# Mixer of a decoder layer: zero products in the first loads, powers of C ahead in the list, and the value projection on split operands in pieces between the scores

## The chip, the cores and the metric

The kernel runs on one core of a Trainium2 chip. The metric is the device time of one execution in microseconds (us). The kernel before takes 971.11 us as the median of three runs (968.80 to 971.95).

Engines are named as in the profile: PE is TensorE, with PEld for its weight loads, DVE is VectorE, ACT is ScalarE, POOL is GpSimd, and SP issues the loads (SPq is its queue).

## The reference

One decoder layer on 256 tokens of 1024 channels, all in float32. Cut to what matters here:

```python
z = x @ w_in                      # 1024 -> [u 512 | q 512 | k 512 | v 512]
# head group A: diagonal complex state space model, 32 groups x 16 channels, 64 states each
lam_bar = exp(lam * dt);  b_bar = ((lam_bar - 1) / lam) * b
states  = scan(a = lam_bar, b = b_bar . u)            # over the 256 tokens
y       = Re(c . states) + d * u
y       = gelu(y);  y = y * sigmoid(y @ w_glu)        # w_glu 512 x 512
# head group B: causal attention, 8 heads x 64
p       = softmax(mask(q k^T / 8))
att     = p @ v
# both groups through one output projection, then residual + layer norm
h       = layernorm(alpha * x + concat(y, att) @ w_out)
# second sublayer (PEER: product-key choice among 128 x 128 one-neuron experts, then their
# values) and a second layernorm: not touched by the change
```

## The kernel before

The work is one stream of instructions per engine. The source writes the mixer (the first 150 us) as short routines, and the list `CFG["order"]` (L46) says in which order they are called: `u`, `q`, `k`, `va`, `vb` are the four projections of x, `par`, `b`, `c0`, `c`, `rt`, `rot` prepare the state space model on DVE, `min` transposes a prepared matrix on PE, `e0`, `e1` are the products that feed the scan, `s0`, `s1` the scan itself, `a0` and `a1` one step each of the attention for the first and the second 128 tokens, `kin`, `o0`, `o1` the products behind the scan, `p0`, `p1` the attention's values, `glu` the gate. A scheduler then places the instructions on each engine, by the order in which they were written and by when it reckons each to be ready, so that routines mix on an engine.

**Products.** A float32 product on PE is two passes, which the trace shows as two records. For the large products the kernel splits an operand into a rounded part `hi` and the rest `lo` (`split`, L67 to L73: a cast on ACT, L71, and a subtraction on DVE, L72) and adds three products of the split parts, one record each. The four projections of x (`tokproj` L158, its products L164; `chproj` L167, its products L175) use plain float32 products; `w_glu` and `w_out` are split.

**Buffers.** Loads of 512 KB go through rings: `raw` (4 buffers), `hi` (3) and `lo` (3), tags that the projections' weight tiles `w` take in turn (L143 to L151). The PSUM banks are in three rings: `pbank`, `sbank` (two banks; names psb) and `abank` (pa).

**The start.** SP issues the small parameters, two of eight channel tiles of x, the first weights and so on (L130 to L139). DVE clears a large matrix `Bbd` (L564) and computes a long chain of small instructions on 128x16 elements. PE begins with `u`.

**Around the scores.** `e0` writes two sbank banks and `e1` two abank banks (L413). DVE ends the ladder of rotations `rot` (L371 to L376), reads the banks (L421 to L426) and scans (L429). PE goes from `e1` to the first half of the value projection (`va`: 8 products of 128x512), then the scores: per head a score (L520) and a mask (L524), a maximum on DVE (L526), an exponential on ACT (L529), a transpose on PE (L534) and a copy on ACT (L536). The second half of the value projection (`vb`) stands among the transposes of the second 128 tokens. Its two sums are copied to `vn` (L587), and `kin` follows (L395).

**The gate.** `glu` multiplies by split `w_glu` (L475 to L477) with the split input `yh` (ACT, L467) and `yl` (DVE, L468), half by half; the output projection (L654) begins with the attention's channels k = 4 to 7 and fills gaps. `w_out` tile 5 is read through the ring like 4 and 6; tiles 0 and 1 take the places `Kin` and `qk` when these are free (L668).

Of the kernel before, what the change touches and what calls it, by code (L numbers as in the profile page):

```python
# [8 lines left out]
F32 = mybir.dt.float32  # L9
F32R = mybir.dt.float32r  # L10
# [31 lines left out]
def f32(ap):  # L42
    return ap.bitcast(F32)


CFG = dict(order='mask zero u par b q min rt rot k e0 e1 s0 va a0 a0 a0 a0 s1 a1 a1 a1 a1 vb c0 c kin p0 o0 p1 o1 glu',  # L46
           glu='VV',
           post='VV',
           yt='AAAAVVVVVVVPVVVV',
# [4 lines left out]
def layer(ctx, tc, I, out, tap=None, upto=None):  # L54
    nc = tc.nc
    V, S, P, PE = nc.vector, nc.scalar, nc.gpsimd, nc.tensor

    const = ctx.enter_context(tc.tile_pool(name="const", bufs=1))
    stream = ctx.enter_context(tc.tile_pool(name="stream", bufs=1))
    RAWB, HIB, LOB = 4, 3, 3  # L60

    def load(src):
        raw = stream.tile([128, 1024], F32, tag="raw", bufs=RAWB, name="raw")
        nc.sync.dma_start(raw, src.rearrange("p a b -> p (a b)") if len(src.shape) == 3 else src)
        return raw

    def split(raw, eng=V, hi=None, lo=None):  # L67
        if hi is None:
            hi = stream.tile([128, 1024], F32R, tag="hi", bufs=HIB, name="hi")
            lo = stream.tile([128, 1024], F32R, tag="lo", bufs=LOB, name="lo")  # L70
        S.copy(hi, raw)  # L71
        eng.tensor_tensor(lo, raw, f32(hi), op=OP.subtract)  # L72
        return hi, lo  # L73
# [26 lines left out]
    def pbank(shape):  # L100
        return ps.tile(shape, F32, tag="w", bufs=4, name="pw")

    def sbank(shape):
        return ps.tile(shape, F32, tag="s", bufs=2, name="psb")
# [6 lines left out]
    with ExitStack() as px:  # L111
# [6 lines left out]
        with ExitStack() as mx:  # L118
# [8 lines left out]
            prm = se.tile([128, 1088], F32, name="prm")  # L127
            x0 = const.tile([128, 2, ND * T], F32, tag="x2", name="x0")
            xT = x0[:, 0].rearrange("p (d t) -> p d t", t=T)
            nc.sync.dma_start(prm[:, 0:48], I["prm"][:, 0:48])  # L130


            for q in range(4):
                nc.sync.dma_start(xT[:, 2 * q:2 * q + 2], I["xT"][:, 2 * q:2 * q + 2, :])
                if q == 0:
                    w0 = stream.tile([128, 1024], F32, tag="raw", bufs=RAWB, name="raw")
                    for k in range(2):
                        nc.sync.dma_start(w0[:, 512 * k:512 * k + 512], I["w_in"][0, :, k, :])
            nc.sync.dma_start(prm[:, 48:], I["prm"][:, 48:])  # L139
            ahead = {(0, 0): w0}  # L140
            spot = [0]

# [1 line left out]
            def w_in(blk, q):  # L144
                if (blk, q) in ahead:
                    return ahead[blk, q]
                t, n = (("raw", RAWB), ("hi", HIB), ("lo", LOB))[spot[0] % 3]
                spot[0] += 1
                w = stream.tile([128, 1024], F32, tag=t, bufs=n, name="w")
                nc.sync.dma_start(w, I["w_in"][blk, :, 2 * q:2 * q + 2, :].rearrange("p a b -> p (a b)"))  # L150
                return w  # L151


            U = se.tile([128, NPAIR, 2, 32], F32, name="U")
            Uv = U.rearrange("p a b c -> p a (b c)")
            qk = sb.tile([128, 2, 4, T], F32, name="qk")

            def tokproj(blk, pt, qs=range(4)):  # L158
                for q in qs:
                    w = w_in(blk, q)  # L160
                    for k in range(2):
                        d = 2 * q + k
                        for b in range(2):
                            PE.matmul(pt[b], xT[:, d, 128 * b:128 * b + 128],  # L164
                                      w[:, 512 * k:512 * k + 512], start=d == 0, stop=d == 7)

            def chproj(blk, scale):  # L167
                pt = [pbank([128, 2, T])[:, 0] for _ in range(4)]
                for q in range(4):
                    w = w_in(blk, q)  # L170
                    for k in range(2):
                        d = 2 * q + k
                        for m in range(4):
                            c = slice(512 * k + 128 * m, 512 * k + 128 * m + 128)
                            mm = PE.matmul(pt[m], w[:, c], xT[:, d], start=d == 0, stop=d == 7)  # L175
                for m in range(4):
                    S.activation(qk[:, blk - 1, m], pt[m], AF.Copy, scale=scale)
                return mm


            pw = sb.tile([128, 40, NPAIR], F32, name="pw")
# [162 lines left out]
            def s5_min():  # L344
                for ri in range(2):
                    for a in range(4):
                        pt = sbank([128, 4, 128])
                        for i in range(4):
                            PE.transpose(pt[:, i], Bbd[:, ri, 4 * a + i].rearrange("p j g -> p (j g)"),
                                         ident)  # L350
                        S.copy(MinT[:, ri, 4 * a:4 * a + 4], pt)

            def s5_c0():
                for i in range(2):
# [204 lines left out]
            M = {}  # L559
            zx = sb.tile([128, 2, NPAIR, NCH], F32, tag="zx", name="zx") if "P" in CFG["post"] else None  # L560

            def do(w):
                if w == "zero":
                    V.memset(Bbd, 0.0)  # L564
                    P.memset(Cbd, 0.0)
                    P.memset(Rt[:, :, 0:1], 0.0)
                    S.activation(Kin, ident[:, None, :].to_broadcast([128, NPAIR, 128]), AF.Copy,
                                 scale=0.0)
                elif w == "u":
                    pu = [abank([128, 512]) for _ in range(2)]  # L570
                    tokproj(0, pu)
                    for b in range(2):
                        V.transpose(U[:, :, b, :], pu[b].rearrange("p (a g) -> p a g", g=32))
                elif w == "q":
                    M["q"] = chproj(1, 0.125)
                elif w == "k":
                    chproj(2, 1.0)
                elif w == "va":

                    pv = M["pv"] = [sbank([128, 512]) for _ in range(2)]  # L580
                    tokproj(3, pv, range(2))
                elif w == "vb":
                    pv = M["pv"]
                    tokproj(3, pv, range(2, 4))
                    M["v"] = vn = sb.tile([128, 2, 512], F32, tag="vn", name="vn")
                    for b in range(2):
                        S.copy(vn[:, b], pv[b])  # L587
                elif w == "par":
                    M["p"] = s5_params()
                elif w == "b":  # L590
                    s5_b(M["p"][0])
                elif w == "c0":
                    s5_c0()
                elif w == "c":
                    s5_c()
                elif w == "rt":
                    s5_rt(M["p"][1])
                elif w == "rot":
                    s5_rot()
                elif w == "min":  # L600
                    with tc.issue_after(M["q"].ins):
                        s5_min()
                elif w == "kin":
                    s5_kin()
                elif w in ("e0", "e1"):
                    M[w] = s5_e(int(w[1]))
                elif w in ("s0", "s1"):
                    if "S" not in M:
                        M["S"] = sb.tile([128, 2, NPAIR, NCH + 1], F32, tag="MinT", name="Sst")
                        P.memset(M["S"][:, :, :, 0:1], 0.0)  # L610
                    s5_scan(int(w[1]), M["e" + w[1]], M["S"])
                elif w in ("o0", "o1"):
                    if "y" not in M:
                        M["y"] = se.tile([128, 4, 2, 4, 32], F32, tag="yT", name="yT")
                    s5_out(int(w[1]), M["S"], M["y"])
                elif w == "mask":
                    masks()
                elif w in ("a0", "a1"):
                    if w not in M:
                        M[w] = attend(int(w[1]))  # L620
                    next(M[w])
                elif w in ("p0", "p1"):
                    values(int(w[1]), M["v"])
                elif w == "glu":
                    glu(M["y"])
                else:
                    raise ValueError(w)
# [28 lines left out]

            W = {}
            for k in (4, 5, 6, 7):
                if k in LATE:
                    r = W3[:, 2 * (k - 6):2 * (k - 6) + 2]  # L660
                    W[k] = split(load(I["w_out"][:, k, :]), V, r[:, 0], r[:, 1])
                else:
                    W[k] = wload(I["w_out"][:, k, :])
                for b in range(1 if k in LATE else 2):
                    out_mm(b, k, W[k])


            for k, t in enumerate(("Kin", "qk")):  # L668
                r = sb.tile([128, 2, 1024], F32R, tag=t, name="W0")
                W[k] = split(load(I["w_out"][:, k, :]), V, r[:, 0], r[:, 1])  # L670
            W2 = sb.tile([128, 4, 1024], F32R, tag="Bbd", name="W2")
            for k in range(2):
# [548 lines left out]
```

## Time and profile before

| | us |
|---|---|
| median of three runs | 971.11 (968.80 to 971.95) |
| profiled execution | 973.51 |
| its span | 971.7 |
| PE busy in the span | 949.5 (98%), mean granted clock 0.984 |
| DVE busy | 705.2 (73%) |
| ACT busy | 546.6 (56%) |
| scores and value projection, from the end of `e1` to the start of `kin` | 60.03 to 97.35 |
| `kin` | 97.35 to 104.46 |

The times of rows are from one profiled execution of 973.51 us, 2.4 above the median. The start of a row is counted from the span's start. A clock of 1.00 is the higher of PE's two levels, 2.4 GHz, and 0.50 the lower, 1.2 GHz. Idle time in square brackets is what an engine waited before the row, and on what. PE is busy or nearly so in almost every slice of the page, so its own work, its clock and its few waits make the time.

### The profile page before, as it was taken

What the parts mean: (1) busy time and instruction counts of PE and PEld (TensorE: products, weight loads), DVE (VectorE), ACT (ScalarE), POOL (GpSimd) and SP (SyncE); (2) the same over time, 40 slices, a digit from 0 to 9 for tenths busy, and PEclk for the clock granted to TensorE, in tenths of its full rate; (3) what the DMA queues carried; (4) which work ended last, traced back from release to release, by engine and by line L of the source; (5) the groups of instructions that cost most, each with busy time, mean ns of one, the idle gap of its engine ahead of it and who ended that gap; (6) DMA issues with size and microseconds to landing.
All of it is one profiled execution on the core that took longest, in us unless ns stands there. A gap on an engine that the chain in (4) does not pass through costs nothing.

```text
span 971.7 us, 15703 instructions
## 1 busy us (share of the span) xinstructions
PE 949.5 (98%) x5774; PEld 825.5 (85%) x5774; DVE 705.2 (73%) x1495; ACT 546.6 (56%) x1059; POOL 21.4 (2%) x25
## 2 busy tenths in 40 slices
PE   7999999999999999999999999999999999999995
PEld 3876977998888888999999999788888878888884
DVE  8974467999888876987889886555555555555556
ACT  3214353557557557987878775455555565555552
POOL 3000003000000000000000000000000000000002
PEclk9996999999999999999999999999999999999998
DMA  8320283356565565444545444566656575656651
GB/s 336 120 66 16 72 264 125 110 182 192 190 192 188 187 193 187 159 158 152 163 141 166 159 154 155 171 197 193 193 194 195 195 264 193 194 194 195 196 195 43
DMA packets 49788, 166.20 MB, mean 171 GB/s; under 512 B 5296, under 2 KB 9392, under 8 KB 49584
## 3 DMA queue, kind: packets, MB, share of 16 engines
q1 hardware_dynamic: 49712, 165.20, 52.6%
q8 instruction: 45, 0.74, 0.3%
q14 instruction: 31, 0.25, 0.1%
HBM read 163.09 MB, written 2.10 MB: 170 GB/s over the span
## 4 chain that ended last, share of the span: by engine, by line
PE 93%; DVE 4%; DMA 1%; issue 1%; ACT 0%; SPq 0%; DVEq 0%; ACTq 0%
PE pw L1068 35%; PE psb L1141 19%; PE pw L864 11%; PE pw L866 6%; PE pw L1016 3%; PE pw L175 3%; PE pa L1141 2%; PE pw L654 2%; PE psb L164 2%; PE pw L867 2%; PE pw L520 1%; PE pa L164 1%; PE pw L395 1%; DMA w<-in_w_in 1%; PE psb L449 1%; DMA tail<-in_ln_g 1%
## 5 line engine op out<-in xcount | busy, mean ns | idle before, releaser
L72 DVE TENSOR_TENSOR lo<-raw,hi 128x1024 fp32r<-128x1024 f32 x195 | 238.4, 1223 | 155.7 <-ACT hi L71 151.4
L71 ACT CAST hi<-raw 128x1024 fp32r<-128x1024 f32 x195 | 205.0, 1052 | 210.9 <-PE pw L1068 162.3
L1068 PE MATMUL pw<-hi,wh 128*128 128x512 f32 x492 | 151.7, 389 | 1.4 <-ACT wh L985 1.4
L1068 PE MATMUL pw<-hi,wl 128*128 128x512 f32 x492 | 152.1, 389 | 0.6 <-DVE wl L986 0.5
L1068 PE MATMUL pw<-lo,wh 128*128 128x512 f32 x492 | 151.9, 389 | 0.0
L1141 PE MATMUL psb<-x,hi 128*128 128x256 f32 x1024 | 133.3, 283 | 0.0
L1141 PEld LDWEIGHTS psb<-x,hi 128*128 128x128 f32 x1024 | 127.4, 192 | 0.0
L864 PE MATMUL pw<-x,hi 128*128 128x512 f32 x448 | 113.5, 392 | 0.0
L1068 PEld LDWEIGHTS pw<-hi,wh 128*128 128x128 f32 x492 | 92.2, 188 | 21.2 <-ACT wh L985 2.3
L1068 PEld LDWEIGHTS pw<-hi,wl 128*128 128x128 f32 x492 | 92.2, 188 | 20.5 <-DVE wl L986 1.5
L1068 PEld LDWEIGHTS pw<-lo,wh 128*128 128x128 f32 x492 | 92.4, 188 | 19.3
L864 PEld LDWEIGHTS pw<-x,hi 128*128 128x128 f32 x448 | 84.2, 188 | 16.4
L79 DVE TENSOR_TENSOR lo<-raw,hi 128x1024 fp32r<-128x1024 f32 x64 | 78.0, 1219 | 15.2 <-ACT hi L78 14.5
L1010 ACT ACTIVATE o<-eq,gL 128x128 f16<-128x128 f16 x256 | 85.4, 438 | 1.0 <-DVE eq L1006 0.9
L1141 PE MATMUL psb<-x,lo 128*128 128x256 f32 x512 | 76.5, 292 | 0.0
L866 PEld LDWEIGHTS pw<-x,lo 128*128 128x128 f32 x512 | 69.8, 190 | 5.0
L866 PE MATMUL pw<-x,lo 128*128 128x256 f32 x512 | 71.4, 282 | 0.0
L78 ACT CAST hi<-raw 128x1024 fp32r<-128x1024 f32 x64 | 67.4, 1054 | 3.7 <-PE pa L1141 2.3
L1141 PEld LDWEIGHTS psb<-x,lo 128*128 128x128 f32 x512 | 65.1, 191 | 0.0
L869 ACT COPY ul<-pw 128x256 f32<-128x256 f32 x64 | 23.8, 371 | 64.4 <-PE pw L867 64.4
L1023 DVE TENSOR_TENSOR act<-pw,act 128x256 f32<-128x256 f32 x124 | 38.3, 350 | 25.6 <-PE pw L1016 25.5
L985 ACT CAST wh<-act 128x256 fp32r<-128x256 f32 x123 | 51.5, 419 | 0.8 <-PE pw L1068 0.8
(310 smaller groups left out, 1166.7 us busy)
## 6 DMA issues: line engine op xcount, KB each, us to landing
raw<-in_u SPq DMA_DIRECT2D x128, 512.0 KB, 3.5
raw<-in_v SPq DMA_DIRECT2D x128, 512.0 KB, 3.5
w<-in_w_in SPq DMA_DIRECT2D x15, 512.0 KB, 8.2
raw<-in_w_q SPq DMA_DIRECT2D x12, 512.0 KB, 3.7
raw<-in_w_out SPq DMA_DIRECT2D x8, 512.0 KB, 4.1
raw<-in_w_q SPq DMA_DIRECT2D x8, 256.0 KB, 3.8
x<-in_xT SPq DMA_DIRECT2D x4, 256.0 KB, 4.8
raw<-in_w_glu SPq DMA_DIRECT2D x2, 512.0 KB, 3.7
```

The costliest lines, as they stand in the source:

```text
L71: S.copy(hi, raw)
L72: eng.tensor_tensor(lo, raw, f32(hi), op=OP.subtract)
L78: S.copy(hi, raw)
L79: return hi, lo, V.tensor_tensor(lo, raw, f32(hi), op=OP.subtract)
L164: PE.matmul(pt[b], xT[:, d, 128 * b:128 * b + 128], w[:, 512 * k:512 * k + 512], start=d == 0, stop=d == 7)
L864: PE.matmul(pt, hi[:, 128 * d:128 * d + 128], x2[:, d], start=d == 0, stop=False)
L866: PE.matmul(pt[:, 0], lo[:, 128 * d:128 * d + 128], xh[:, d], start=False, stop=False)
L985: S.copy(wh, of_tile(half, i))
L1010: S.activation(o2[:, 1, i // 2, :, i % 2], eq[:, i // 2, :, i % 2], AF.Copy, scale=gL[:, t0 + i:t0 + i + 1])
L1023: V.tensor_tensor(a, gp[:, :, HALF // 2 * h:HALF // 2 * h + n], a, op=OP.mult)
L1068: PE.matmul(acc[b][c], x[:, tk], w[:, 512 * c:512 * c + 512], start=first and j == 0, stop=last and j == 2)
L1141: PE.matmul(pt, w[:, 128 * d:128 * d + 128], x[:, d], start=n == 0 and d == 0, stop=n == 2 and d == ND - 1)
```

## The change

Six edits, all in the mixer. From the first expert product on, PE's order is the same but for names.

- **Zero products.** DVE clears a 128x512 tile `warm` ahead of everything, and PE multiplies it twice into a bank that nothing reads, ahead of `u`. The loads are put in another order: one tile of x, half of the first weights, the parameters, the next tile, the other half, then x and the weights in turn; the larger part of the parameters comes after them.
- **`c0 c` (powers of C)** stand ahead of `e0` in the list rather than behind `vb`.
- **`xs`** splits x (four casts on ACT, four subtractions on DVE) and the weights of the value projection (four casts, four subtractions L72).
- **`v`** is called eight times, between the steps of the attention, and each call adds six products of split operands (L212), for two sums of 128x512. The 16 plain products go.
- **`w_out` tile 5** gets the buffer of `qk`, and tiles 0 and 1 other places.
- The splits of `w_glu`, which stood among the projections, come later on DVE.

```diff
-CFG = dict(order='mask zero u par b q min rt rot k e0 e1 s0 va a0 a0 a0 a0 s1 a1 a1 a1 a1 vb c0 c kin p0 o0 p1 o1 glu',
+CFG = dict(order='mask zero u par b q min rt rot k c0 c xs e0 e1 s0 v v a0 v a0 v a0 a0 v s1 a1 v a1 v a1 a1 v kin p0 o0 p1 o1 glu',
...
-            nc.sync.dma_start(prm[:, 0:48], I["prm"][:, 0:48])
-            for q in range(4):
-                nc.sync.dma_start(xT[:, 2 * q:2 * q + 2], I["xT"][:, 2 * q:2 * q + 2, :])
-                if q == 0:
-                    w0 = stream.tile([128, 1024], F32, tag="raw", bufs=RAWB, name="raw")
-                    for k in range(2):
-                        nc.sync.dma_start(w0[:, 512 * k:512 * k + 512], I["w_in"][0, :, k, :])
-            nc.sync.dma_start(prm[:, 48:], I["prm"][:, 48:])
+            w0 = stream.tile([128, 1024], F32, tag="raw", bufs=RAWB, name="raw")
+            warm = se.tile([128, 512], F32, tag="yT", name="warm")
+            V.memset(warm, 0.0)
+            pt = pbank([128, 512])
+            for _ in range(2):
+                PE.matmul(pt, warm[:, 0:128], warm, start=True, stop=True)
+            for k in range(2):
+                nc.sync.dma_start(xT[:, k], I["xT"][:, k, :])
+                nc.sync.dma_start(w0[:, 512 * k:512 * k + 512], I["w_in"][0, :, k, :])
+                if k == 0:
+                    nc.sync.dma_start(prm[:, 0:48], I["prm"][:, 0:48])
...
+            for q in range(1, 4):
+                nc.sync.dma_start(xT[:, 2 * q:2 * q + 2], I["xT"][:, 2 * q:2 * q + 2, :])
+                ahead[0, q] = w_in(0, q)
+            nc.sync.dma_start(prm[:, 48:], I["prm"][:, 48:])
...
+            def xsplit():
+                for q in range(4):
+                    d = slice(2 * q, 2 * q + 2)
+                    S.copy(mixh[:, d], xT[:, d])
+                    V.tensor_sub(mixl[:, d], xT[:, d], f32(mixh[:, d]))
+                for q in range(4):
+                    own = [se.tile([128, 1024], F32R, tag=t, name="wv") for t in ("yT", "dU")] if q == 2 else ()
+                    with tc.issue_after(M["min"].ins):
+                        M["wv", q] = split(load(I["w_in"][3, :, 2 * q:2 * q + 2, :]), V, *own)
+            def vproj(pt):
+                for q in range(4):
+                    hi, lo = M["wv", q]
+                    for k in range(2):
+                        d, c = 2 * q + k, slice(512 * k, 512 * k + 512)
+                        for b in range(2):
+                            tk = slice(128 * b, 128 * b + 128)
+                            for j, (x, w) in enumerate(((mixh, hi), (mixl, hi), (mixh, lo))):
+                                PE.matmul(pt[b], x[:, d, tk], w[:, c], start=d == 0 and j == 0,
+                                          stop=d == 7 and j == 2)
+                        yield
...
-                elif w == "va":
-                    pv = M["pv"] = [sbank([128, 512]) for _ in range(2)]
-                    tokproj(3, pv, range(2))
-                elif w == "vb":
-                    pv = M["pv"]
-                    tokproj(3, pv, range(2, 4))
-                    M["v"] = vn = sb.tile([128, 2, 512], F32, tag="vn", name="vn")
-                    for b in range(2):
-                        S.copy(vn[:, b], pv[b])
+                elif w == "v":
+                    if "pv" not in M:
+                        M["pv"] = [sbank([128, 512]) for _ in range(2)]
+                        M["vproj"], M["left"] = vproj(M["pv"]), 8
+                    next(M["vproj"])
...
-                if k in LATE:
+                if k == 5:
+                    r = sb.tile([128, 2, 1024], F32R, tag="qk", name="W5")
+                    W[k] = split(load(I["w_out"][:, k, :]), V, r[:, 0], r[:, 1])
+                elif k in LATE:
...
-            for k, t in enumerate(("Kin", "qk")):
-                r = sb.tile([128, 2, 1024], F32R, tag=t, name="W0")
+            for k in range(2):
+                r = sb.tile([128, 2, 1024], F32R, tag="Kin", name="W1") if k else W3[:, 0:2]
```

PE in the kernel before, at the end of `e1` (L413): the plain products of the value projection (L164), then score, mask and score by turns.

```order
L413 MATMUL pa<-U,MinT 128x64 x16
L164 MATMUL psb<-w,x_93 128x512 [waits DMAHW3_49,DVE_49,PE_49]
L164 MATMUL psb<-w,x_93 128x512 [waits DVE_49,PE_49]
L164 MATMUL psb<-w,x_93 128x512 x2
L164 MATMUL psb<-w,x_93 128x512 [waits DMAHW4_49]
L164 MATMUL psb<-w,x_93 128x512 x3
L520 MATMUL pw<-qk 128x128 [waits Activation_49]
L524 LDWEIGHTS identb
L524 MATMUL pw<-mb,identb 128x128
L520 MATMUL pw<-qk 128x128 [waits Activation_49]
```

PE in the changed kernel, at the same place (`e1` is L449, scores L556, masks L560, the value projection L212):

```order
L449 MATMUL pa<-U,MinT 128x64 x16
L556 MATMUL pw<-qk 128x128 [waits Activation_49]
L560 LDWEIGHTS identb
L560 MATMUL pw<-mb,identb 128x128
L556 MATMUL pw<-qk 128x128 [waits Activation_49]
L212 MATMUL psb<-hi,mixh 128x512 [waits DVE_49,PE_49,Pool_49]
L212 MATMUL psb<-hi,mixl 128x512
L212 MATMUL psb<-lo,mixh 128x512
L212 MATMUL psb<-hi,mixh 128x512
L212 MATMUL psb<-hi,mixl 128x512
L212 MATMUL psb<-lo,mixh 128x512
L212 MATMUL psb<-hi,mixh 128x512 [waits DVE_49]
```

The eight plain products are gone from here; the first of the new ones stands two scores behind `e1`, and it waits for DVE, which has to have read the two banks of `e0` (psb) first.

DVE in the kernel before, at the end of the rotations (L375, L376) and at the readings of the banks (L421 to L424):

```order
L375 TENSOR_TENSOR big_116<-rot 128x512
L376 TENSOR_TENSOR rot<-big_115,big_116 128x16x32 [waits DVE_49]
L72 TENSOR_TENSOR lo<-raw,hi 128x1024 [waits DMAHW0_49,DMAHW5_49,PE_49,Activation_49]
L421 TENSOR_TENSOR big_113<-psb,rot 128x512 [waits PE_49]
L425 TENSOR_TENSOR big_116<-psb,rot 128x512 [waits DVE_49]
L422 TENSOR_TENSOR big_114<-psb,rot 128x512 [waits PE_49]
L424 TENSOR_TENSOR big_115<-psb,rot 128x512
```

DVE in the changed kernel, at the same place (rotations L411, L412, readings L457, L458, L460, L461):

```order
L411 TENSOR_TENSOR big_128<-rot 128x512
L72 TENSOR_TENSOR lo<-raw,hi 128x1024 [waits DMAHW4_49,DMAHW2_49,Activation_49]
L412 TENSOR_TENSOR rot<-big_127,big_128 128x16x32 [waits DVE_49]
L72 TENSOR_TENSOR lo<-raw,hi 128x1024 [waits DMAHW6_49,DMAHW5_49,Activation_49]
L72 TENSOR_TENSOR wv<-raw,wv 128x1024 [waits DMAHW6_49,Activation_49]
L457 TENSOR_TENSOR big_125<-psb,rot 128x512 [waits PE_49]
L72 TENSOR_TENSOR lo<-raw,hi 128x1024 [waits DMAHW7_49,DMAHW1_49,Activation_49]
L458 TENSOR_TENSOR big_126<-psb,rot 128x512 [waits DVE_49,PE_49]
L460 TENSOR_TENSOR big_127<-psb,rot 128x512
L459 TENSOR_TENSOR big_125<-big_125,big_126 128x512 [waits DVE_49]
L461 TENSOR_TENSOR big_128<-psb,rot 128x512
```

Four subtractions L72, the splits of the value projection's weights, stand about the end of the rotations and between the readings, where one stood before. Further ahead on DVE, the four subtractions of x stand in the chain of small instructions, ahead of the rotations.

PE in the kernel before, at the second half of the gate (L475 to L477), ahead of it the last products of the output projection (L654) that are ready:

```order
L654 MATMUL pw<-hi,mixh 128x512 x2
L654 MATMUL pw<-hi,mixl 128x512 x2
L654 MATMUL pw<-lo,mixh 128x512 x2
L475 MATMUL psb<-yh,hi 128x256 [waits Activation_49]
L475 MATMUL psb<-yh,hi 128x256
L476 MATMUL psb<-yl,hi 128x256 [waits DVE_49]
L477 MATMUL psb<-yh,lo 128x256
```

PE in the changed kernel, at the same place (gate L511 to L513, output projection L693; W_1078 is the split tile 5):

```order
L693 MATMUL pw<-hi,mixh 128x512 x2
L693 MATMUL pw<-hi,mixl 128x512 x2
L693 MATMUL pw<-lo,mixh 128x512 x2
L693 MATMUL pw<-W_1078,mixh 128x512 x2
L693 MATMUL pw<-W_1078,mixl 128x512
L511 MATMUL psb<-yh,hi 128x256 [waits Activation_49]
L511 MATMUL psb<-yh,hi 128x256
L693 MATMUL pw<-W_1078,mixl 128x512
L693 MATMUL pw<-W_1078,mixh 128x512 x4
L693 MATMUL pw<-W_1078,mixl 128x512
L512 MATMUL psb<-yl,hi 128x256 [waits DVE_49]
L513 MATMUL psb<-yh,lo 128x256
```

Nine products of tile 5 have come to stand about the two waits of the gate's second half, three ahead of the first and six ahead of the second.

## Rows read from the trace of the kernel before

**Rows 1.** The page, the chain that ended last, by engine.

```profile
PE 93%; DVE 4%; DMA 1%; issue 1%; ACT 0%; SPq 0%; DVEq 0%; ACTq 0%
```

**Rows 2.** Windows, the mixer: length, PE, PEld, DVE, ACT, POOL, clock, DMA share, GB/s.

```profile
35.47:40.42 4.95, 4.95 (x39) 4.22 (x38) 4.88 (x14) 4.05 (x9) 0.00 (x0) 1.00 0.34 107
52.94:60.03 7.09, 7.09 (x65) 7.09 (x64) 4.72 (x8) 1.47 (x3) 0.00 (x0) 1.00 0.45 150
60.03:67.05 7.02, 7.02 (x19) 2.91 (x18) 6.76 (x11) 0.00 (x0) 0.15 (x1) 1.00 0.01 1
67.05:70.45 3.40, 3.40 (x19) 2.34 (x18) 1.45 (x3) 1.26 (x6) 0.00 (x0) 1.00 0.52 154
70.45:90.90 20.45, 20.45 (x65) 13.11 (x65) 10.67 (x16) 6.60 (x27) 0.00 (x0) 0.50 0.01 1
97.35:104.46 7.11, 7.11 (x66) 6.91 (x65) 4.30 (x9) 3.23 (x7) 0.00 (x0) 1.00 0.29 84
121.05:128.45 7.40, 5.78 (x35) 4.67 (x35) 6.12 (x15) 6.14 (x10) 0.86 (x1) 1.00 0.77 216
128.45:131.90 3.45, 3.45 (x19) 3.45 (x18) 2.65 (x5) 2.54 (x5) 0.00 (x0) 0.51 0.81 260
```

**Rows 3.** Chain of waits in order of time: start, us, work.

```profile
60.20 6.92 PE psb L164 x16
67.12 0.41 PE pw L520 x2
67.53 0.16 PE pw L524
72.97 1.15 PE pw L520 x4
...
74.13 0.22 PE pw L524
92.40 0.22 PE pa L534 x2
133.67 6.41 PE pw L654 x28
```

**Rows 4.** Timeline of DVE from 28 to 60 us: start, us, instruction, idle before it.

```profile
28.39 0.96 DVE L323 TENSOR_TENSOR Bbd<-big,big 64x768 f32<-64x768 f32 x1
51.17 0.69 DVE L376 TENSOR_TENSOR rot<-big,big 128x512 f32<-128x512 f32 x1
51.78 1.22 DVE L72 TENSOR_TENSOR lo<-raw,hi 128x1024 fp32r<-128x1024 f32 x1
54.87 0.69 DVE L421 TENSOR_TENSOR big<-psb,rot 128x512 f32<-128x512 f32 x1 [1.87 <-PE psb L413]
```

**Rows 5.** Timeline of DVE, PE and its weight loads, the start.

```profile
1.66 3.47 DVE L564 MEMSET Bbd<- 128x4096 f32 x1 [1.66 <-PEq L1210]
5.71 5.32 PE L164 MATMUL pa<-raw,x 128*128 128x512 f32 x8 [5.71 <-DMA raw<-in_w_in]
7.55 0.34 PEld L164 LDWEIGHTS pa<-raw,x 128*128 128x128 f32 x1 [0.52 <-issue]
8.40 0.34 PEld L164 LDWEIGHTS pa<-raw,x 128*128 128x128 f32 x1 [0.52 <-issue]
9.58 0.19 PEld L164 LDWEIGHTS pa<-raw,x 128*128 128x128 f32 x1 [0.24 <-issue]
10.01 0.19 PEld L164 LDWEIGHTS pa<-raw,x 128*128 128x128 f32 x1 [0.24 <-issue]
11.26 10.57 PE L164 MATMUL pa<-w,x 128*128 128x512 f32 x24 [0.23 <-DMA w<-in_w_in]
```

**Rows 6.** Timeline of PE and DVE at the gate's second half.

```profile
125.95 1.23 DVE L72 TENSOR_TENSOR W<-raw,W 128x1024 fp32r<-128x1024 f32 x1
126.70 0.50 PE L475 MATMUL psb<-yh,hi 128*128 128x256 f32 x2 [0.99 <-ACT yh L467]
127.84 0.39 PE L476 MATMUL psb<-yl,hi 128*128 128x256 f32 x1 [0.63 <-DVE yl L468]
```

More of the change, by code (lines that the diff above doesn't have):

```diff
@@ L156, in layer, with tokproj @@
             qk = sb.tile([128, 2, 4, T], F32, name="qk")
-            def tokproj(blk, pt, qs=range(4)):
-                for q in qs:
+            def tokproj(blk, pt):
+                for q in range(4):
                     w = w_in(blk, q)
@@ L178, in chproj @@
                 return mm
+            def xsplit():
[8 more added lines that the diff above has]
+            def vproj(pt):
+                for q in range(4):
+                    hi, lo = M["wv", q]
[7 more added lines that the diff above has]
+                        yield
             pw = sb.tile([128, 40, NPAIR], F32, name="pw")
@@ L350, in s5_min @@
                                          ident)
-                        S.copy(MinT[:, ri, 4 * a:4 * a + 4], pt)
+                        M["min"] = S.copy(MinT[:, ri, 4 * a:4 * a + 4], pt)
             def s5_c0():
@@ L577, in do @@
                     chproj(2, 1.0)
-                elif w == "va":
-                    pv = M["pv"] = [sbank([128, 512]) for _ in range(2)]
-                    tokproj(3, pv, range(2))
-                elif w == "vb":
-                    pv = M["pv"]
-                    tokproj(3, pv, range(2, 4))
-                    M["v"] = vn = sb.tile([128, 2, 512], F32, tag="vn", name="vn")
-                    for b in range(2):
-                        S.copy(vn[:, b], pv[b])
+                elif w == "xs":
+                    xsplit()
+                elif w == "v":
[3 more added lines that the diff above has]
+                    next(M["vproj"])
+                    M["left"] -= 1
+                    if not M["left"]:
+                        M["v"] = vn = sb.tile([128, 2, 512], F32, tag="vn", name="vn")
+                        for b in range(2):
+                            S.copy(vn[:, b], M["pv"][b])
                 elif w == "par":
```

## The prediction

> **What bounds the kernel now.** I read the page first: the chain that ended last is PE for 93% [rows 1], so time can come only out of PE's work, its clock or its waits. I then cut the mixer into windows, since one average hides the stages. Six stretches of those shown run at the higher level; two do not. From 70.45 to 90.90, the scores and transposes, PE is busy all 20.45 us but the clock is 0.50, and 128.45 to 131.90 has 0.51 [rows 2]. The stretch ahead of the first holds scores and masks alone; ahead of the second PE is idle for 1.62 of 7.40 us [rows 2], 0.99 and 0.63 of it in the two waits of the gate [rows 6]. The chain of waits gives prices at both levels: a score of two passes and its mask take 0.41 and 0.16 us at the higher one, two scores and their mask 1.15 and 0.22 at the lower [rows 3].
>
> **The start.** The first product of `u` waits for the loads until 5.71 us, and is first at the lower level: weight loads of 0.34 us follow each other by 0.85 us, later ones of 0.19 by 0.43 [rows 5]. A 128x512 clear of `warm` takes an estimated 0.43 (3.47 for eight times the elements [rows 5]), so the zero products can start at about 2.1 us and are four records of 0.85, to 5.5. If the clock is then up, `u`'s 32 records take 32 x 0.43, some 14 us, and `u` ends at 19.8 where it ended at 21.82 (11.26 and 10.57 [rows 5]). I take 2.0 us earlier; bounds 0 to 2.4. But it does not reach the end, for the reason below.
>
> **DVE ahead of the scores.** The powers of C move in the list, but on DVE they already stood among the rotations; they cost nothing. What comes in is four subtractions of x, 128x512, at 0.60 apart (a row's 0.69 overlaps the next: 51.17 to 51.78 [rows 4]), 2.4 us, and four splits at 1.22 [rows 4], where one was. The clear's 0.43 I put at nothing; at most 0.4. DVE's chain there ran to 53.0 and then waited 1.87 us for `e0` [rows 4]. Now the last rotation, whose end was 51.78, ends 2.4 + 1.2 later, at 55.4; two more splits bring the first reading of a bank to 57.8, where it was 54.87. Behind it come 0.6 for the reading, 1.2 for the fourth split, 0.6 and 0.7 for two more readings: 60.9. Only then is the first bank free for the value projection. PE, 2.0 earlier, ends `e1` at 58.0 (60.03 in the row's edge [rows 2]), does two scores and a mask (1.0) and stands from 59.0. It waits 1.9 us. So the start's gain is spent here, and whether the zeros raise the clock hardly matters. Bounds of the wait: 0, if DVE swallows the subtractions in gaps, to 5, if it has everything, or a load is late. The matrix that PE transposes first was written by 29.35 (28.39 and 0.96 [rows 4]); plus 2.4, that is still ahead of 33.5, when `q` now ends, since PE takes the transposes at 35.47 [rows 2].
>
> **From 60.9 to the end of `kin`.** At the higher level:
> - the value projection, 48 products of one record at 6.41/28 = 0.229 [rows 3]: 11.0. Before, 16 products of two records cost 2 x 6.92 = 13.8 [rows 3];
> - the scores of the first 128 tokens that are left, six at 0.41 + 0.16 and a mask: 3.65;
> - eight heads of the second 128 tokens. No row shows one at the higher level: half of 1.15 + 0.22 is 0.69, two scores of 0.41 and a mask 0.99 [rows 3]; I take 0.80: 6.4;
> - 24 transposes, 0.11 each [rows 3], and up to the 0.20 of an exposed weight load [rows 5]; I take 0.14: 3.4;
> - `kin`, 7.1 [rows 2].
>
> The sum is 31.55, so `kin` would end at 92.45. To this comes the clock. The wait of 1.9 us is longer than the idle time that preceded the fall at 128.45, and that fall lasted 3.45 us [rows 2], half of which is lost: 1.7. In the second 128 tokens, scores and transposes follow each other with one piece of V only; there I count half of another such fall, 0.85. `kin` ends at 95.0 where it ended at 104.46: 9.4 gained.
>
> Is PE still the bound there? DVE's work from 52.94 to 90.90 was 4.72 + 6.76 + 1.45 + 10.67 = 23.6 [rows 2]; from 57.8, with the fourth split, it ends at 82.6, some 2 to 3 us ahead of `kin` on PE. The two splits of `w_glu` and two of `w_out` then fall behind it, 4.9 us beside `kin`'s 7.1, in which DVE had 4.30 busy [rows 2]: about full, but the products behind `kin` need the last of its results only at its end. I charge nothing; up to 1 us if not hidden.
>
> On those transposes a page speaks against me. In rows, 32 of the 39 records from 35.47 to 40.42 are transposes of this kind, and the clock stayed at 1.00 in them and in the next stretch shown [rows 2]. The Trainium skill, "TensorE: Matmul & The Clock Gate", Part 4: PE-mode transpose, says that a transpose does not count as PE work for the clock, so that full speed does not engage. By this rule the clock would not hold among transposes and scores, which is the first rival below; this trace does not agree with it. Also, "Perfetto Trace Analysis" of the Trainium skill, Engine Utilization, halves the output rate for float32 passes; by that a plain 128x512 product would cost 0.46 and the split would lose 3.7 us. The trace has two records of 0.43 for one [rows 3], so it saves 2.8.
>
> **The gate.** PE's first wait in the second half was 0.99 [rows 6]; three products of tile 5 (0.69) now stand ahead of it, which leaves 0.3. The second was 0.63 [rows 6]; `yl` comes 1.2 later, since one more split stands ahead of it on DVE, and six products (1.37) are ahead of it on PE: 0.46. That is 0.86 less idle time, and the products are only brought forward. With half the idle time the fall behind it, 1.7, may go; I count three quarters, 1.3. Together 2.2; bounds 0 (the splits late) to 2.6.
>
> **The sum.** 9.4 + 2.2 = 11.6 us of the profiled execution's 973.5, so 961.9; the median lies 2.4 below that execution, so 959.5. Its own range: 956 (one fall less, the wait half) to 963.5 (a fall more, the gate 1 us).
>
> **The rivals.**
> - *The clock does not hold.* The pieces of V do not keep it up, or a transpose does not count: as much time at the lower level as before, 20.45. For it: before, scores alone let it fall [rows 2]. Against it: V is 11 of 24 us of the stage, spread out, and large products ran at 1.00 wherever PE did not wait. From 92.45, 10.2 are lost: 12.0 - 10.2 + 2.2 = 4.0 gained, 967.1. Chance 13%.
> - *Never a fall.* For it: before `u`'s second weights PE waited too, and went on at 0.43 per record [rows 5]. 12.0 + 2.2 gives 956.9; without the wait 955. 17%.
> - *DVE decides the stage.* It has no gaps for the subtractions, or the weights' splits wait for a load; PE stands 5 us at its first piece, 3.1 more, and a little more of the lower clock: 963. 12%.
> - *Slower: V's products run at the lower level with the rest.* The wait of 1.9 us lets the clock fall, and the mixture does not raise it until `kin`: 24.45 us at the higher level become 48.9, `kin` ends at 116.9, 12.4 late; with 2.2 back at the gate that is 10.2 slower, 981. It decides once more than 14.2 of the 24.45 us (28.4 us in the trace) are at the lower level. Against it: the three stretches of large products at 1.00 [rows 2]. 4%.
> - *No change.* The scores' chain of maximum, exponential and transpose sets the stage, and PE's saved time turns into waits. Against it: PE had no idle time at all in 70.45 to 90.90 [rows 2], and the chain's engines were busy for half of it. 4%.
>
> **How the numbers follow.** The forecast has 50%. A difference under 0.3%, 2.9 us, cannot be told from none here: faster is below 968.2. Faster takes the forecast, 17%, 12% and most of the first rival: 0.89. Within 0.3%: no change and the rest of the first: 0.07. Slower: 0.04. The range for 8 in 10 leaves out the slow case, no change and half of the first rival, and goes down past the case without a fall or a wait: 953.5 to 967.5.
>
> **What would show it.** In the changed kernel's windows, the clock from the first piece of V to `kin`: near 1.00 with one or two falls of some 3 us, or 0.50 for most of it. On PE's timeline, the idle time ahead of the first L212, released by DVE: 1 to 3 us. On DVE's, the first reading (L457) near 57.8. `kin` (L431) ending near 95. At the gate, waits of 0.3 and 0.5 us and no stretch at half clock behind them. At the start, weight loads of 0.19 from the first real product on, and `u` ending near 19.8. I am wrong if `kin` ends after 100, or if the time of the stages behind 155 us differs.

## The result, and the profile after

The changed kernel takes 959.32 us as the median of five runs (958.93 to 960.77), the kernel before 971.01 (968.80 to 971.95). The ratio is 0.9881, with a 95% interval of 0.9869 to 0.9893. The profiled execution took 960.77 us, with a span of 959.0 and a mean clock of 0.996, where before had 0.984.

The windows of the changed kernel, from `e1` to the end of the gate; columns as in [rows 2]:

```profile
51.10:58.31 7.21, 7.21 (x66) 7.12 (x64) 7.21 (x9) 2.34 (x6) 0.00 (x0) 1.00 0.38 106
58.31:59.94 1.63, 1.06 (x6) 0.71 (x6) 1.63 (x4) 0.00 (x0) 0.15 (x1) 0.97 0.92 256
59.94:63.10 3.16, 3.16 (x8) 2.51 (x9) 3.16 (x5) 0.00 (x0) 0.00 (x0) 0.50 0.79 294
63.10:72.28 9.18, 9.18 (x43) 6.17 (x41) 7.50 (x14) 3.51 (x10) 0.00 (x0) 0.99 0.01 2
72.28:80.09 7.81, 7.81 (x42) 5.44 (x41) 7.46 (x11) 3.50 (x15) 0.00 (x0) 1.00 0.01 2
80.09:86.48 6.39, 6.39 (x40) 4.62 (x39) 3.79 (x7) 4.04 (x14) 0.00 (x0) 1.00 0.00 0
86.48:94.62 8.14, 8.14 (x70) 7.21 (x69) 7.14 (x13) 6.08 (x14) 0.00 (x0) 1.00 0.63 192
111.20:120.45 9.25, 8.59 (x50) 6.93 (x49) 7.73 (x16) 7.98 (x12) 0.85 (x1) 1.00 0.80 219
120.45:124.14 3.69, 3.69 (x29) 3.33 (x28) 2.45 (x4) 2.40 (x7) 0.00 (x0) 1.00 0.91 271
```

The 20.45 us at 0.50 of [rows 2] are gone; one stretch of 3.16 us at 0.50 is left, at the first products of V, the value projection. `kin` ends at 94.62 where it ended at 104.46: 9.84 us. In the gate PE is idle for 0.66 us, where it was 1.62 of 7.40 [rows 2], and no stretch at 0.51 follows.

The timeline of PE: the start, the first product of V, and the two waits of the gate.

```profile
1.45 3.78 PE L137 MATMUL pw<-warm 128*128 128x512 f32 x4 [1.45 <-DVE warm L134]
5.03 1.98 PE L174 MATMUL pa<-raw,x 128*128 128x512 f32 x4
7.57 1.95 PE L174 MATMUL pa<-raw,x 128*128 128x512 f32 x4 [0.56 <-DMA raw<-in_w_in]
9.46 10.54 PE L174 MATMUL pa<-w,x 128*128 128x512 f32 x24
...
59.94 0.77 PE L212 MATMUL psb<-hi,mixh 128*128 128x512 f32 x1 [0.57 <-DVE big L460]
60.50 0.63 PE L212 MATMUL psb<-hi,mixl 128*128 128x512 f32 x1
...
116.88 0.50 PE L511 MATMUL psb<-yh,hi 128*128 128x256 f32 x2 [0.28 <-ACT yh L503]
...
119.15 0.39 PE L512 MATMUL psb<-yl,hi 128*128 128x256 f32 x1 [0.38 <-DVE yl L504]
```

The zeros do what they are for: the first real products follow each other by some 0.43 from 5.03 on, where they began at 0.85 [rows 5]. The level is read from this rate alone, since the clock column of the windows has 1.00 at the start of both kernels. But PE then waits for the loads at 7.57, and `u` ends near 19.9 (21.82 before). The first product of V waits 0.57 for DVE. The gate's waits are 0.28 and 0.38 where they were 0.99 and 0.63 [rows 6].

DVE at the readings of the banks:

```profile
53.90 0.69 DVE L412 TENSOR_TENSOR rot<-big,big 128x512 f32<-128x512 f32 x1
54.51 1.22 DVE L72 TENSOR_TENSOR lo<-raw,hi 128x1024 fp32r<-128x1024 f32 x1
55.64 1.22 DVE L72 TENSOR_TENSOR wv<-raw,wv 128x1024 fp32r<-128x1024 f32 x1
56.78 0.69 DVE L457 TENSOR_TENSOR big<-psb,rot 128x512 f32<-128x512 f32 x1
57.38 1.22 DVE L72 TENSOR_TENSOR lo<-raw,hi 128x1024 fp32r<-128x1024 f32 x1
...
59.11 0.68 DVE L460 TENSOR_TENSOR big<-psb,rot 128x512 f32<-128x512 f32 x1
```

The first reading is at 56.78 (54.87 before [rows 4]), and the first bank is free when L460 ends, at 59.8.

### The profile page after: what moved, and what is told of

Same layout as the page of the kernel before. It is cut to its first block, busy times and chain, and to the rows that moved or that the text cites. A ratio compares the mean times of both kernels' runs of the same rounds, so it can differ in the third digit from the quotient of the medians.

```text
span 959.0 us, 15765 instructions
## 1 busy us (share of the span) xinstructions
PE 941.5 (98%) x5794; PEld 822.9 (86%) x5794; DVE 711.2 (74%) x1504; ACT 551.2 (57%) x1067; POOL 21.4 (2%) x25
## 4 chain that ended last, share of the span: by engine, by line
PE 88%; DVE 10%; issue 1%; DMA 1%; ACT 0%; DVEq 0%; ACTq 0%; SPq 0%
PE pw L1110 35%; PE psb L1183 20%; PE pw L906 11%; PE pw L908 6%; PE pw L1058 3%; PE pa L1183 2%; PE pw L909 2%; PE pw L693 1%; PE psb L212 1%; PE pw L556 1%; PE pw L431 1%; PE psb L485 1%; PE pa L798 1%; DMA tail<-in_ln_g 1%; PE pw L581 1%
## 5 line engine op out<-in xcount | busy, mean ns | idle before, releaser
L72 DVE TENSOR_TENSOR lo<-raw,hi 128x1024 fp32r<-128x1024 f32 x197 | 241.0, 1224 | 152.4 <-ACT hi L71 150.8
```

## The experiments

Each set shared its runs of the kernel before, on one chip, a different chip for each set; a set's ratios and medians are compared with each other. In the first set (e1 to e4) before had 972.53 us, in the second (e5 to e7 and the changed kernel again) 972.15, in the third (e8 to e10 and the changed kernel a third time) 971.28. The changed kernel had 959.31 (ratio 0.9873, 0.9857 to 0.9888) in the second and 959.10 (0.9879, 0.9864 to 0.9894) in the third; for e1 to e4 its ratio stands in for a run beside them.

**V ahead of the scores (e1).**

```diff
-... e0 e1 s0 v v a0 v a0 v a0 a0 v s1 a1 v a1 v a1 a1 v kin ...
+... e0 e1 s0 v v v v v v v v a0 a0 a0 a0 s1 a1 a1 a1 a1 kin ...
```

> The changed kernel with all eight pieces of the value projection ahead of the scores; every instruction stays, only places change. Theory (the gain is the clock that V's products hold up among the scores): the scores and transposes, some 13.5 us at the higher level, fall to the lower one after the first 3 us as in the kernel before, cost 9 to 10 us more, and the time is 968 to 970. Rival (the gain is V's shorter products and the gate, wherever V stands): 959 to 961.

968.28 us (966.67 to 970.28), ratio 0.9960 (0.9945 to 0.9975): 9 us more than the changed kernel, by moving instructions alone. Its windows:

```profile
60.00:71.50 11.50, 11.50 (x51) 9.21 (x51) 11.50 (x18) 3.01 (x4) 0.00 (x0) 1.00 0.20 77
71.50:75.00 3.50, 3.50 (x21) 2.21 (x20) 3.50 (x7) 2.28 (x8) 0.00 (x0) 0.97 0.01 2
75.00:78.00 3.00, 3.00 (x11) 2.03 (x11) 1.93 (x4) 0.84 (x4) 0.00 (x0) 0.50 0.42 113
78.00:92.00 14.00, 14.00 (x49) 9.33 (x50) 5.01 (x8) 6.18 (x22) 0.00 (x0) 0.50 0.04 14
```

V's products run at 1.00, then the scores and transposes are by themselves, and the clock falls after some 3.7 us of them (V ends at 71.1, and 0.97 in the second window puts the fall at 74.8) and stays down. PE is busy all the time. So the gain among the scores is the clock, and the place of V's products makes it.

**V among the first half's scores alone (e9).**

```diff
-... s0 v v a0 v a0 v a0 a0 v s1 a1 v a1 v a1 a1 v kin ...
+... s0 v v a0 v v a0 v v a0 v v a0 s1 a1 a1 a1 a1 kin ...
```

> The changed kernel with all eight pieces of V among the scores of the first 128 tokens, none among the scores and transposes of the second 128. Theory (scores and transposes alone let the clock fall after some 3 us, in whichever half they stand): a stretch at 0.50 in the second half, 5 to 10 us long, 2.5 to 5 us more, ratio 0.990 to 0.993. Rival (a stage that was kept up until then stays up, or the transposes keep it): ratio 0.987 to 0.989, clock 1.00.

965.02 us (964.81 to 966.39), ratio 0.9938 (0.9925 to 0.9952): 5.9 more than the changed kernel, a little over the range of the theory. The windows behind V's last product:

```profile
74.52:78.77 4.25, 4.25 (x27) 3.14 (x27) 4.25 (x6) 2.25 (x7) 0.00 (x0) 0.98 0.23 42
78.77:92.44 13.67, 13.67 (x53) 9.08 (x52) 6.24 (x10) 6.27 (x20) 0.00 (x0) 0.51 0.19 66
```

Again some 4 us of scores and masks after the last large product, and then the lower level, ahead of the first transpose of this stretch (78.77). In the changed kernel a stretch of scores and transposes of that length, 80.09 to 84.25, lies between two pieces of V and stays at 1.00.

**Zeros between the scores of the kernel before (e7).** Products are added that change no sum, in nine pieces of four. So they are 36 and not the 32 by which the expectation reckoned; the trace has 36 of their weight loads and 33 of the products.

```diff
-... va a0 a0 a0 a0 s1 a1 a1 a1 a1 vb ...
+... va f a0 f a0 f a0 f a0 s1 f a1 f a1 f a1 f a1 f vb ...
...
+                elif w == "f":
+                    if "fz" not in M:
+                        M["fz"] = Kin.rearrange("p a b -> p (a b)").bitcast(BF)
+                    fz = M["fz"]
+                    for i in range(4):
+                        PE.matmul(M["pv"][i % 2], fz[:, 0:128], fz[:, 0:512], start=False, stop=False)
```

> The kernel before with 32 products of zeros (128x512, of the still cleared Kin read as bf16) put between its scores and added into V's sums, which they leave as they are: 6.8 us more work at the higher clock, nothing less. Theory (the gain among the scores is the clock): the 20.45 us at 0.50 vanish, 10.2 less and 6.8 more, 967 to 969 where before is 971, ratio 0.995 to 0.998. Rival (the clock among the scores is not set by such products, or the gain came from V's shorter products): 6.8 to 13.6 more, ratio 1.007 to 1.014.

972.46 us (970.95 to 974.48), ratio 1.0009 (1.0000 to 1.0018): neither. The windows:

```profile
67.29:88.41 21.12, 21.02 (x114) 12.69 (x116) 12.16 (x20) 9.35 (x35) 0.00 (x0) 1.00 0.17 51
88.41:96.63 8.22, 8.22 (x23) 3.59 (x23) 1.48 (x3) 3.24 (x7) 0.00 (x0) 1.00 0.00 0
```

Two pieces of zeros and a pair of scores on its chain of waits:

```profile
67.29 0.81 PE psb L587 x3
...
69.25 0.86 PE psb L587 x4
...
77.05 0.64 PE pw L520 x4
```

The clock is 1.00 throughout, so idle arithmetic holds it as well as V does. A zero takes 0.215 (0.86 for four), so 36 are some 7.7 us of added work. Yet `kin` begins at 96.63, 0.72 earlier than before (97.35 [rows 2]), and V's first product 0.1 later. So the lower level had cost some 8.5, not the 10.2 that half of 20.45 would be, and the zeros use up nearly all that they bring back. A pair of scores shows the same: 1.15 at the lower level [rows 3], 0.64 here and in the changed kernel.

This profile shows one thing more. The gate is that of the kernel before, and PE's two waits there are 1.17 and 0.46, no shorter in sum than before (0.99 and 0.63 [rows 6]); but no fall follows. The output projection ends 43.9 us behind `kin` (147.70 and 103.80), where before it was 45.2 (149.64 and 104.46). So the fall at the gate costs some 1.3, and it does not follow from the waits alone.

**V as plain products (e3).** No splits of x or of the weights; 16 products of two records at the same places.

```diff
- for j, (x, w) in enumerate(((mixh, hi), (mixl, hi), (mixh, lo))):
-     PE.matmul(pt[b], x[:, d, tk], w[:, c], ...)
+ PE.matmul(pt[b], xT[:, d, 128 * b:128 * b + 128], w[:, 512 * k:512 * k + 512], ...)
```

> The changed kernel with V's pieces as plain float32 products of x and the weights, no splits of either: 16 products of two records, 13.8 us for 11.0, at the same places between the scores. Theory (any large products hold the clock; the split saves 2.8 but costs the wait of 0.57 and the 1.5 of the fall behind it): 959.5 to 961.5, clock near 1.00 through the scores. Rival (only the split pieces hold the clock, or the split is what pays): 963 to 968.

960.04 us (959.81 to 960.77), ratio 0.9876 (0.9860 to 0.9892), as the theory said. Its V stands right behind `e1` and waits for nothing, the clock holds, and 58.11 to 87.36 has no idle time:

```profile
58.11:87.36 29.25, 29.25 (x125) 15.98 (x125) 21.73 (x35) 12.02 (x42) 0.15 (x1) 1.00 0.13 37
```

Within the intervals it equals the changed kernel, but all four of its times lie above the four of e2 beside it (958.92 to 959.69, 0.7 less in the median), which has the split. So of the 2.8 that the split saves on PE some 0.7 may be left, at the edge of what can be told; V starts at 58.11 here and at 59.94 in the changed kernel, so most of it goes into the later start.

**No zeros (e2).** The clear and the two products go; the loads keep their new order.

> The changed kernel without the clear of warm and without the two zero products; the order of the loads stays new. Theory (the first real products run at the lower level while they would otherwise wait for the second half of the weights, and DVE decides the start of V): 959.2 to 959.8, no difference. Rival (the zeros give what u gained, 1.7 us): 960.8 to 961.3.

959.32 us (958.92 to 959.69), ratio 0.9868 (0.9853 to 0.9884): no difference. PE at the start, and at V's first product:

```profile
4.04 5.65 PE L169 MATMUL pa<-raw,x 128*128 128x512 f32 x8 [4.04 <-DMA raw<-in_w_in]
9.52 10.46 PE L169 MATMUL pa<-w,x 128*128 128x512 f32 x24
...
60.13 0.47 PE L207 MATMUL psb<-hi,mixh 128*128 128x512 f32 x1 [0.78 <-DVE big L455]
60.44 0.40 PE L207 MATMUL psb<-hi,mixl 128*128 128x512 f32 x1
```

The slow first products fill just the time in which the kernel with zeros waits for the second half of the weights. And here V's first product waits longer than in the changed kernel, 0.78, but no fall follows.

**The old start in the changed kernel (e8).** No zeros, loads in the old order.

> The changed kernel with the old start: no zeros, the loads in the old order; e1 then ends about 2 us later, near 60.3. Theory (DVE sets the start of V, so the start's gain is spent in the wait there): V starts at about 61.2 without a wait, 1.2 us later than in the changed kernel, and the fall of 1.5 may be absent: 959.0 to 960.6, ratio 0.9870 to 0.9885. Rival (the start's gain arrives, as it did in the kernel before, where it was 4): 961.3 to 963.3, ratio 0.9892 to 0.9915.

961.09 us (960.88 to 962.62), ratio 0.9901 (0.9886 to 0.9916): 2.0 more than the changed kernel beside it. The theory, the one of the prediction, is wrong here; the ratio is in the rival's range, the time 0.2 under it. PE between `e1` and V, the window from V's first product on, and DVE:

```profile
60.98 0.49 PE L546 MATMUL pw<-qk 64*128 64x128 f32 x2
...
62.18 0.47 PE L202 MATMUL psb<-hi,mixh 128*128 128x512 f32 x1
```

```profile
62.18:72.00 9.82, 9.82 (x46) 6.98 (x47) 9.49 (x16) 3.61 (x10) 0.00 (x0) 1.00 0.29 114
```

```profile
56.76 0.68 DVE L447 TENSOR_TENSOR big<-psb,rot 128x512 f32<-128x512 f32 x1
59.61 1.22 DVE L72 TENSOR_TENSOR lo<-raw,hi 128x1024 fp32r<-128x1024 f32 x1 [2.17 <-ACT hi L71]
...
61.36 0.68 DVE L450 TENSOR_TENSOR big<-psb,rot 128x512 f32<-128x512 f32 x1
```

The scores begin at 60.98 (58.31 in the changed kernel) and V at 62.18 (59.94), 2.24 later: of 2.67 only 0.4 were waiting time. The fourth split waits 2.17 us on DVE here, behind a late load and ACT's cast, which is another part of the changed order; PE does not get there before 62.0 in any case.

The profiles alone would say less than the medians. V runs at 1.00 here, as the theory allowed, without the fall of 1.5 us that the changed kernel's profiles have, so `kin` ends at 95.30, only 0.7 behind the changed kernel's 94.6, and the profiled execution (960.88) is shorter than that of the changed kernel beside it (961.70). The 2.0 stands between the medians. It agrees with the 2.24 at V's start if the changed kernel's median execution has no fall; the runs of the changed kernel below speak for that, but no trace shows it.

**The new start in the kernel before (e6).**

> The kernel before with only the new start: zero products and the new order of the loads. Theory (in the kernel before nothing on DVE holds PE behind e1, so what u gains arrives): 1.6 to 2.0 us less, ratio 0.9979 to 0.9984. Rival (the start is hidden there too, or the time goes back into the stretch at the lower clock): ratio 0.9995 to 1.0005.

967.81 us (966.40 to 969.01), ratio 0.9959 (0.9945 to 0.9974): 4.3 less, more than either. The windows of its scores:

```profile
64.70:69.90 5.20, 5.20 (x29) 3.64 (x30) 3.11 (x6) 2.14 (x11) 0.00 (x0) 1.00 0.36 101
69.90:87.50 17.60, 17.60 (x59) 11.25 (x58) 8.89 (x14) 5.74 (x25) 0.00 (x0) 0.52 0.00 1
```

V's first product starts 2.4 earlier, at 57.76 (60.20 [rows 3]), which arrives. Further, the fall comes 5.2 us after V's first half instead of 3.4 and the stretch at the lower level is some 17 us long (17.60 at a mean of 0.52) instead of 20.45 [rows 2]; `kin` begins 3.86 earlier. Why the fall comes later is open.

**Tile 5 as before (e5).** Tile 5 goes back to the ring, and tiles 0 and 1 to their old places.

```diff
-                if k == 5:
-                    r = sb.tile([128, 2, 1024], F32R, tag="qk", name="W5")
-                    W[k] = split(load(I["w_out"][:, k, :]), V, r[:, 0], r[:, 1])
-                elif k in LATE:
+                if k in LATE:
...
-            for k in range(2):
-                r = sb.tile([128, 2, 1024], F32R, tag="Kin", name="W1") if k else W3[:, 0:2]
+            for k, t in enumerate(("Kin", "qk")):
+                r = sb.tile([128, 2, 1024], F32R, tag=t, name="W0")
```

> The changed kernel with w_out tile 5 back in the ring and tiles 0 and 1 back at Kin and qk; the rest stays changed. Theory (tile 5 fills the two waits of the gate and keeps the clock up): waits of 1.0 and 0.6 us and a stretch of 3 us at 0.50 are back, 2.2 us more, ratio 0.990 to 0.9915. Rival (the gate's gain comes from the other edits, such as the splits of w_glu elsewhere): no more than 0.5 us, ratio 0.988 to 0.989.

961.50 us (960.58 to 963.73), ratio 0.9905 (0.9889 to 0.9921): 2.2 more than the changed kernel beside it, as the theory said. PE's waits, and the windows behind them:

```profile
115.35 0.50 PE L511 MATMUL psb<-yh,hi 128*128 128x256 f32 x2 [1.06 <-ACT yh L503]
...
116.41 0.38 PE L512 MATMUL psb<-yl,hi 128*128 128x256 f32 x1 [0.55 <-DVE yl L504]
```

```profile
116.00:119.00 3.00, 2.59 (x15) 2.59 (x16) 2.27 (x4) 1.94 (x5) 0.00 (x0) 0.72 0.74 238
119.00:122.00 3.00, 3.00 (x21) 3.00 (x20) 2.90 (x5) 2.22 (x4) 0.00 (x0) 0.72 0.67 217
```

Both waits are back at their old length [rows 6], and a stretch at the lower level behind them as well: 0.72 over these 6 us is the lower level for some 3.4 of them, as in the kernel before.

**The last weight split later (e4), and that without zeros (e10).**

```diff
-... xs e0 e1 s0 v v a0 v a0 ...
+... xs e0 e1 s0 a0 xw v v v a0 ...
```

`xs` now splits x and the first two quarters of the weights, `xw` the other two; one step of the scores stands ahead of V, whose first three pieces stand together.

> The changed kernel with the last of the four weight splits behind the scan's first half on DVE and one more step of the scores ahead of V, so that PE finds V's bank free: no wait of 0.57. Theory (the wait lets the clock fall for 3.3 us): no fall at V's first products, 957.3 to 958.2. Rival (the thin products of e1 and the first scores let it fall, wait or not): the fall stays, 958.7 to 959.5.

958.48 us (957.62 to 959.50), ratio 0.9857 (0.9841 to 0.9874): between the ranges of theory and rival, 0.8 under e2 in the median, with overlapping times and intervals. Between `e1` and V, PE has no wait, and the clock does not fall; V's products follow each other at 0.23:

```profile
59.48 0.23 PE L561 MATMUL pw<-mb,identb 128*128 128x128 bf16 x1
59.52 0.48 PE L213 MATMUL psb<-hi,mixh 128*128 128x512 f32 x1
59.84 0.39 PE L213 MATMUL psb<-hi,mixl 128*128 128x512 f32 x1
60.07 0.39 PE L213 MATMUL psb<-lo,mixh 128*128 128x512 f32 x1
```

> A candidate that might beat the changed kernel: the later weight split of the run e4 and no zero products. Theory (the zeros are worth nothing, the later split removes the wait and the fall at V's first products): 957.3 to 958.5 where the changed kernel has 959.3, ratio 0.9850 to 0.9865. Rival (the wait was worth nothing either): as the changed kernel, 0.987 to 0.988.

958.70 us (957.57 to 958.86), ratio 0.9867 (0.9853 to 0.9882). All five of its times lie below all five of the changed kernel beside it (958.98 to 961.70), but the intervals of the ratios overlap: 0.4 us less in the median, at the edge of what can be told, and again between theory and rival.

**The changed kernel twice more.**

> The changed kernel once more, to stand beside the others. If the fall of the clock at V's first products belongs to the kernel, this profile shows it again (0.50 from about 60 to 63 us). If it comes in some executions only, as the longer wait without a fall in the kernel without zeros suggests, it may be absent, with a span some 1.5 to 1.9 us shorter. Ratio to the kernel before 0.9870 to 0.9890 either way.

> The changed kernel a third time, for the comparison on one chip: ratio 0.987 to 0.989. The fall at V's first products stood in both profiles so far; a third with it would say that it belongs to this kernel, one without it that it comes in some executions.

Both profiles show the fall at V's first products again, after waits of 0.45 and 0.67 us. Each of the three times, the profiled execution was the longest (960.77, 960.23 and 961.70), and the shortest were 958.93, 958.70 and 958.98. In the three profiles `kin` ends at 94.6 to 94.7 and 863.8 to 865.3 us follow. An execution like the median of the third time (959.10, a span of 957.3) would have only 862.7 left behind a `kin` that ends at 94.6; behind one at 93.1, without the fall, it would have 864.2. So the fall belongs to this kernel, but probably not to all its executions, the median ones among them; this is argued, not shown.

## Why the prediction was right, and where it was not

The time was 959.32 for 959.5. The two larger terms, the scores and the gate, hold; the term for the start does not, and that the total fits so closely is luck in part. The forecast took 11.6 from the profiled execution, to 961.9, and 2.4 more to come to the median. The profiled execution was 960.77, 1.1 less than forecast, and stood 1.45 above its median, not 2.4, 1.0 the other way. Of the 1.1, 0.4 are at `kin` and 0.7 behind the output projection, where the two spans differ (822.1 and 821.4); the other profiles here scatter as much there (820.8 to 822.7), so the sign that the stages behind would differ did not come. Point by point:

- **The scores.** Forecast: `kin` ends at 95.0, 9.4 gained; measured 94.62 and 9.84. That the clock makes most of it is shown by e1, e9 and e7: the same work in other places loses it, other work in the same places holds it.
- **The gate.** Forecast 2.2; the output projection ends 12.03 us earlier (137.61 for 149.64), 2.19 more than `kin` did, and e5 alone gives back 2.2. The waits came as forecast, 0.28 and 0.38 for 0.3 and 0.46. Of the 2.2, 0.86 were put on the waits and 1.3 on the fall; e7, with the old waits and no fall, parts them into 0.9 and 1.3. But e5 has the fall with the waits and e7 the waits without the fall, so the idle time does not decide it alone.
- **The start: the step that failed.** "So the start's gain is spent here" was wrong: the wait at V's first product was 0.57, not 1.9. Taken out of the changed kernel, the start costs 2.0 in the median (e8). Two sizes were off. DVE freed the bank at 59.8, not 60.9: the last rotation ended 2.73 later than before, not 3.6. Of this one more split takes 1.13, and 1.6 are left for the four subtractions of x and all else that moved ahead of it, where 2.4 was reckoned. In e2, where DVE's order up to the subtractions is that of the kernel before, the instruction behind them starts 2.0 later (19.82 for 17.79), though each of them lasts 0.68. And the scores began at 58.31 rather than 58.0. Since the wait hardly binds, what PE gains ahead of it reaches V: 2.24 (e8). In the profiled executions the fall behind the wait takes 1.5 of that back.
- That **the zeros hardly matter** was right (e2), with a wrong reason: not DVE behind them hides them, but the loads of the first weights in front.
- **The work from V to `kin`** was put at 31.55 us. The chain of waits of the changed kernel from 59.94 to 94.62, 34.68 us, by line (L212 V, L556 scores, L431 `kin`, L570 transposes, L560 masks):

```profile
by line: PE psb L212 38.2%; PE pw L556 23.6%; PE pw L431 21.2%; PE pa L570 10.9%; PE pw L560 6.1%
```

  V has 13.25, of which 1.5 are the fall and 11.75 the work, for 11.0; scores and masks 10.3 for 10.05 (of which the 3.65 is 3.58 by its own prices); transposes 3.8, so 0.16 each, for 3.4; `kin` 7.35 for 7.1. In all 1.65 too little was forecast. V began 0.96 earlier than forecast, and the clock cost 1.05 less. Together that is 0.36 early, 94.62 for 95.0: the end of `kin` was hit by errors of opposite sign.
- **The clock's price.** One fall of 3.16 us came, for one and a half of 3.45. That the lower level doubles every time was too much; e7 puts the loss in the 20.45 us at some 8.5, not 10.2. So the first rival, priced by halving the 20.45, was priced some 1.7 too high.
- **The split of V**, put at 2.8 less on PE, is worth 0.7 at most that can be told in the end (e3 against e2). e1 fits this: its 4.2 us below the kernel before are no more than the start's 2.0 and the gate's 2.2.

Not settled: why the fall at V's first products comes after waits of 0.45 to 0.67 in the changed kernel and not after 0.78 and 0.91 in e2 and e1, why the gate's fall is absent in e7, nor why e6's fall comes late. No run separated transposes from scores, so whether a transpose counts for the clock, which the Trainium skill ("TensorE: Matmul & The Clock Gate", Part 4: PE-mode transpose) denies, stays open as well: in e9 the clock fell among scores and masks, ahead of the first transpose, and the transposes behind, among scores, did not bring it back.

## What to carry to other kernels

Where PE is busy and still at the lower clock, large products that have to be done anyway, spread between the thin ones, give the time back without a change of the work; a bunch of them ahead of the thin ones does not. To price a wait of one engine for another, look also at what the waited-for engine absorbs: here four subtractions of 0.68 us, put into a chain of small instructions, delayed it by 2.0 and not by 2.7. A forecast that fits the end of a stage may hide errors of opposite sign; take one edit out to see. And a profile is one execution: where falls of the clock come in some executions and not in others, compare medians as well.

## What was not expected of the hardware

Products of zeros held the granted clock at 1.00 as well as real ones did: some 7.7 us of them between the scores cost next to nothing (e7, ratio 1.0009, 1.0000 to 1.0018). The lower clock made the stretch of scores and transposes some 1.7 times as long (20.45 us for 20.45 - 8.5, about 12), not twice. And PE's waits alone did not decide whether the clock fell: 1.62 us of them at the gate had a fall of 3.45 us behind them before, 1.63 in e7 none.
